# Moving every tap of a 31-tap depthwise convolution to the tensor engine, on its four groups of 32 columns

## The chip, the cores and the metric

The kernel runs on one core of one Trainium2 chip. A core has five engines with queues of their own: the tensor engine (PE, whose weight loads the profile lists apart as PEld), the vector engine (DVE), the scalar engine (ACT), the general engine (POOL) and the engine that only issues transfers (SP). The metric is device time in microseconds (us), and less is better.

## The reference

Two blocks run one after the other on 256 tokens of width 1024 (a state space mixer, a feed-forward part, an attention, a feed-forward part), and then a hybrid layer: its projections feed a low-rank attention and a convolution branch, and an output projection joins both. A layer of routed experts follows. The change touches the convolution branch of the hybrid layer alone, with 512 channels, 256 tokens and 16 learned tokens ahead of them:

```
CONV_CH = 512
CONV_K = 31
def conv_group(a, b, conv_w, conv_b, g_ln, b_ln):
    h = a * jax.nn.sigmoid(b)
    h = lax.conv_general_dilated(h, conv_w[:, None, :].astype(h.dtype), window_strides=(1,),
                                 padding=[(CONV_K - 1, 0)],
                                 dimension_numbers=('NWC', 'WIO', 'NWC'),
                                 feature_group_count=CONV_CH) + conv_b
    h = layernorm(h, g_ln, b_ln)
    return jax.nn.silu(h)
```

So each channel is a sum of 31 shifted copies of itself, each copy times a weight of that channel. Everything is in 32-bit floats.

## The kernel before

Weights stream from HBM in pieces of 128x1024 by SP (`weight`, L120). Each piece is split by ACT (L128) and DVE (L129) into two parts of type float32r, and a product with it is three products on PE (`mm_a`, L138 to L141, and `mm_b`, L143 to L147). Small products are plain f32: the trace shows each of these as two records on PE, one behind the other, each with a weight load.

The hybrid layer is `mix2` (L782). The 512 channels are four blocks `f` of 128 channels, one channel on each partition. `ab(f)` makes two items: the second puts `a * sigmoid(b)` into the tile `cu`, 30 zeros ahead of 272 tokens (L805 to L812). Then the 31 taps:

- `taps_pe` (L816) does some of them on PE: ACT writes the identity times a column of weights into a 128x128 tile `dg` (L821), and PE multiplies it with `cu`, shifted (L822). The tuple `PE_TAPS = (4, 4, 6, 31)` says how many for each block, 45 in all. ACT takes the sum out of PSUM with the bias into `cT` (L825).
- `taps_v` (L827) does the other 79 on DVE, one multiply-add of 128x256 each (L829).

The low-rank attention (`queries`, `key_values`, `attn_items`) goes head by head: `scores` (L964) on PE, a scaled minimum on DVE (L968), exponentials on ACT (L972, L973), `flip` (transposes on PE, L981, taken out by ACT, L983), `values` (L989). `attn_items` gives 50 items (16 of each of these three and two `attn_done`). `conv_done(t)` transposes `cT` to tokens on partitions and starts the layer norm. `norm_later` and `rstd_of` raise to the power -1/2 on POOL (L859, L154). `to_T` (L171) transposes the normed rows for `out_proj`, whose eight items `o` take the attention's rows in the first four and the convolution's in the last four.

In the attention of the block before, `scores` (L724) works on heads of 64 rows each: the two heads of a pair lie both on rows 0 to 63 or both on rows 64 to 127, and pairs on the one and the other half follow each other. The products of the expert router's scores (L1106) come four heads at a time on one half.

The code's order is a list with priorities: `run` emits items one after the other, `weave` spreads a list of side items between others by their number, and `defer` puts a step behind the items that follow. A planner then orders each engine's queue at compile time by that priority and by when it reckons an instruction's inputs to be there. So in the trace the instructions of neighbouring items are mixed. Each engine then works through its own queue in order. The order of the layer is written at its end:

```
run(low_rank() + B[0])
weave([queries] + B[1] + [key_values], C[0])
weave(S, B[2] + C[1] + B[3] + C[2])
load_gain("ffn2_g")
run(C[3])
flush()
o = out_proj(A["w_out2"], KD, mT, keep_tiles(sb, 3, "qT2"))
conv_done(0)
conv_done(1)
run(o[:4])
```

Here `B[f]` is `ab(f)`, `C[f]` the items of the convolution of block `f` (four taps each), and `S` the items of the attention.

Of the kernel before, what the change touches and what calls it, by code (L numbers as in the profile page):

```python
# [32 lines left out]
PE_TAPS = (4, 4, 6, 31)  # L33
# [13 lines left out]
for _n, _c in (("ssd_cw", 24 * 4), ("ssd_cb", 24), ("ffn_cw", 2 * FF * 3), ("ffn_cb", 2 * FF), ("c2w", 4 * CONV_K),  # L47
               ("c2b", 4), ("fox_qg", 1), ("fox_kg", 1), ("dt_bias", 1), ("a_log", 1), ("b_f", 1)):
    _cols(_n, _c)
# [17 lines left out]
def tile_body(ctx, tc, A, out):  # L67
# [13 lines left out]
    # ---- constants  # L81
# [35 lines left out]
    # ---- weights: load a piece, split it exactly in two parts of 12 significant bits  # L117
# [69 lines left out]
    def sum_sq(t, c, o, src, eps):  # L187
        # mean of squares of a row, in two halves
# [30 lines left out]
    def both_norms(t, c, acc):  # L219
        # the residual times the first block's last gain, the means of squares of both, and from these  # L220
        # 1 / rms of the first norm and the product of that with 1 / rms of the norm that follows it
# [12 lines left out]
    def keep_tiles(pool, n, *names):  # L234
        # made when first written; names: slots of tiles that are not read any more by then
        return [lambda name=name: pool.tile([P, 2, PIECE], F32R, name=name, bufs=1)
                for name in [*names, *(f"keep{j}" for j in range(n - len(names)))]]

    def out_proj(src, nk, yT, keep, fin=residual):
        """The last pieces are kept, so that the first tokens are done before the others."""  # L240
# [32 lines left out]
    def defer(f, n=1):  # L273
        """Emit a step after the n-th of the items that follow."""
        late.append([n, f])
# [8 lines left out]
    def flush():  # L284
        while late:
            tick()
# [6 lines left out]
    def weave(items, side, behind=False):  # L293
        """Emit a list of steps with a list of smaller ones spread between them, by their costs.

        behind: VectorE takes up the smaller ones only behind the split of the step's weights.
        """
# [17 lines left out]
    def causal(ps, acc, taps, cw, cb):  # L315
        # causal convolution along the tokens; the last tap has no shift
# [25 lines left out]
    def b_first(src, xT, pool, evac):  # L342
        """A block that begins on the first tokens while the others are still on their way."""
# [10 lines left out]
        def turn(f):  # L354
            # two of its four blocks of columns, columns on partitions
# [8 lines left out]
    def row_parts(pool, rows, name):  # L364
        # a table that is there twice, at partitions 0 and 32: its first part at 0, its second at 32
# [6 lines left out]
    def rowbc(ps, rows, r, more=None):  # L372
        # one row of a table in two parts, on all partitions; more: a tile to add
# [19 lines left out]
    # ---- layer 0: state space mixer  # L393
    def ssd():
        with ExitStack() as es:
# [47 lines left out]
            # large and negative where the position read comes after the position written  # L443
# [32 lines left out]
            def xs_items(g):  # L476
                # inputs of the recurrence, tokens on partitions
# [23 lines left out]
            def chain(g):  # L501
                hs = slice(8 * g, 8 * g + 8)
                # decay between every two positions of a chunk, transposed, times the masked products of B and C
# [21 lines left out]
                def state():  # L525
                    # state after the first chunk, read by the second
# [97 lines left out]
    def fox():  # L624
        with ExitStack() as es:
# [46 lines left out]
            # cum is minus the reference's sum  # L672
# [42 lines left out]
            def attend(hg):  # L715
# [3 lines left out]
                def scores(i, pr):  # L719
# [8 lines left out]
                    # minus the scores, and minus their maximum  # L728
# [53 lines left out]
    def mix2():  # L782
        with ExitStack() as es:
# [14 lines left out]
            # convolution branch: some of the taps on the tensor engine, as diagonal matrices  # L798
            cT = sb.tile([P, 4, T], F32, name="cT")
            U, CP = {}, {}  # L800

            def ab(f):
                pre = []

                def second():  # L805
# [4 lines left out]
                    U[f] = sb.tile([P, TM + CONV_K - 1], F32, name=f"cu{f}")  # L810
                    nc.vector.memset(U[f][:, :CONV_K - 1], 0.0)
                    nc.vector.tensor_tensor(U[f][:, CONV_K - 1:], pre[0], sg, op=OP.mult)  # L812
# [3 lines left out]
            def taps_pe(f, j0, j1):  # L816
                if j0 == 0:
                    CP[f] = ps_mm.tile([P, 512], F32, name="mm")[:, :T]
                dg = sb.tile([P, j1 - j0, P], F32, name="dg", bufs=2)
                for j in range(j0, j1):  # L820
                    nc.scalar.activation(dg[:, j - j0, :], ident, AF.Copy, scale=col("c2w", f * CONV_K + j))  # L821
                    nc.tensor.matmul(CP[f], lhsT=dg[:, j - j0, :], rhs=U[f][:, NM + j:NM + j + T], start=(j == 0),  # L822
                                     stop=(j == PE_TAPS[f] - 1))
                if j1 == PE_TAPS[f]:
                    nc.scalar.activation(cT[:, f, :], CP[f], AF.Identity, bias=col("c2b", f))  # L825

            def taps_v(f, j0, j1):  # L827
                for j in range(j0, j1):
                    nc.vector.scalar_tensor_tensor(cT[:, f, :], U[f][:, NM + j:NM + j + T], col("c2w", f * CONV_K + j),  # L829
                                                   cT[:, f, :], op0=OP.mult, op1=OP.add)  # L830

            def conv_items(f):
                n = PE_TAPS[f]
                return ([lambda j=j: taps_pe(f, j, min(j + 4, n)) for j in range(0, n, 4)]
                        + [lambda j=j: taps_v(f, j, min(j + 4, CONV_K)) for j in range(n, CONV_K, 4)])

            # low-rank query and key-value parts, tokens on partitions
# [13 lines left out]
            def norm_later(src, dst, g, n, then, half=False):  # L851
                # half: the source is twice the row that is meant
# [543 lines left out]
```

## Time and profile before

| what | value |
|---|---|
| median of 3 runs | 1768.36 us (1768.04 to 1769.67) |
| span of the profiled execution, first to last instruction | 1767.2 us |
| what lies around that span, as the difference from the median | 1.16 us |
| PE busy in it | 1728.7 us (98%) |
| DVE busy in it | 1244.6 us (70%) |
| ACT busy in it | 973.6 us (55%) |
| POOL busy in it | 35.2 us (2%) |

No time of its own is recorded for the profiled execution beside its span, so the difference from the median stands for what lies around it. A busy PE is not a PE at its peak: a record lasts longer than the distance to the next, since matmuls are pipelined. What one costs in a row of equal ones is read from the distance between their starts: the timeline merges equal neighbours, and (length of the merged row minus the length of one record) divided by (their number minus one) is that distance.

### The profile page before, as it was taken

How to read it: one execution, taken by the hardware profiler on the slowest of the kernel's cores; microseconds unless marked ns; L12 is line 12 of the kernel's file. 1: busy time of each engine (PE TensorE's matmuls, PEld its weight loads, DVE VectorE, ACT ScalarE, POOL GpSimd, SP SyncE). 2: the span in 40 equal slices, each digit the busy share in tenths (PEclk: the TensorE clock that was granted, in tenths of full speed). 3: DMA queues.
4: the chain of work that ended last, by engine and by line, in shares of the span. 5: the costliest groups of instructions: out<-in, count | busy, mean ns of one | idle time of the engine just before them, and what ended most of it. 6: DMA issues, size and time to landing. Idle time of an engine off the chain costs nothing.

```text
span 1767.2 us, 28831 instructions
## 1 busy us (share of the span) xinstructions
PE 1728.7 (98%) x11035; PEld 1536.4 (87%) x11035; DVE 1244.6 (70%) x2516; ACT 973.6 (55%) x1425; POOL 35.2 (2%) x45
## 2 busy tenths in 40 slices
PE   7999999999999999999999999999999999999998
PEld 6978779987777899878979999999999988888886
DVE  5777667765755677667877999977667666666665
ACT  5778546544465565457854544555555544444443
POOL 0000000000110000000000000000000000000000
PEclk9999999999999999999999999999999999999999
DMA  5534346665454465654245676754454577777774
GB/s 192 175 104 144 119 144 181 189 200 181 131 167 132 125 186 183 204 185 141 80 166 172 214 225 224 224 179 140 142 156 134 167 252 237 237 237 238 238 237 156
DMA packets 87578, 315.29 MB, mean 178 GB/s; under 512 B 9984, under 2 KB 10368, under 8 KB 87312
## 3 DMA queue, kind: packets, MB, share of 16 engines
q1 hardware_dynamic: 80352, 290.36, 52.8%
q10 hardware_dynamic: 7088, 23.09, 3.5%
q8 instruction: 86, 1.41, 0.3%
q14 instruction: 52, 0.43, 0.1%
HBM read 295.59 MB, written 17.83 MB: 177 GB/s over the span
## 4 chain that ended last, share of the span: by engine, by line
PE 91%; DVE 4%; ACT 1%; issue 1%; DMA 1%; POOL 1%; SPq 0%; DVEq 0%; POOLq 0%; ACTq 0%
PE mm L1254 20%; PE mm L139 13%; PE mm L141 13%; PE mm L140 13%; PE mm L146 7%; PE mm L145 7%; PE mm L147 7%; PE pst L1212 5%; DVE lo L129 1%; PE pst L171 1%; PE pst L546 1%; PE pst L724 1%; PE pst L375 1%; PE pst L377 1%; PE po L749 1%
## 5 line engine op out<-in xcount | busy, mean ns | idle before, releaser
L129 DVE TENSOR_TENSOR lo<-raw,hi 128x1024 fp32r<-128x1024 f32 (+1 forms) x492 | 599.9, 1220 | 341.7 <-PE mm L141 112.9
L128 ACT ACTIVATE hi<-raw 128x1024 fp32r<-128x1024 f32 (+1 forms) x492 | 519.3, 1057 | 526.0 <-PE mm L140 242.1
L139 PE MATMUL mm<-xT,hi 128*128 128x256 f32 (+1 forms) x1968 | 562.6, 286 | 1.2 <-DVE cacc L320 1.2
L141 PE MATMUL mm<-xT,lo 128*128 128x256 f32 (+1 forms) x1968 | 557.1, 283 | 1.5 <-DVE lo L129 1.5
L140 PE MATMUL mm<-xT,hi 128*128 128x256 f32 (+1 forms) x1968 | 552.0, 281 | 0.0
L139 PEld LDWEIGHTS mm<-xT,hi 128*128 128x128 f32 x1968 | 373.0, 190 | 5.0 <-issue 2.3
L141 PEld LDWEIGHTS mm<-xT,lo 128*128 128x128 f32 x1968 | 370.7, 188 | 2.6 <-DVE lo L129 2.2
L140 PEld LDWEIGHTS mm<-xT,hi 128*128 128x128 f32 x1968 | 371.8, 189 | 0.5
L1254 PE MATMUL mm<-hi,xT 128*128 128x512 f32 x992 | 270.0, 393 | 0.0
L1254 PEld LDWEIGHTS mm<-hi,xT 128*128 128x128 f32 x992 | 186.3, 188 | 42.6
L1254 PE MATMUL mm<-lo,xT 128*128 128x512 f32 x496 | 154.8, 393 | 0.0
L1254 PEld LDWEIGHTS mm<-lo,xT 128*128 128x128 f32 x496 | 93.1, 188 | 21.7 <-DVE lo L129 0.3
L145 PE MATMUL mm<-hi,xT 128*128 128x512 f32 (+1 forms) x240 | 96.3, 408 | 3.9 <-ACT xT L133 3.8
L1212 PE MATMUL pst<-oo 128*128 128x128 bf16 x768 | 99.4, 297 | 0.0
L147 PE MATMUL mm<-hi,xT 128*128 128x512 f32 (+1 forms) x240 | 95.0, 397 | 2.1 <-DVE xT L134 2.1
L146 PE MATMUL mm<-lo,xT 128*128 128x512 f32 (+1 forms) x240 | 96.1, 400 | 0.7 <-DVE lo L129 0.6
L1212 PEld LDWEIGHTS <-oo 128*128 128x128 bf16 x768 | 83.3, 118 | 3.4
L1214 ACT ACTIVATE G<-pst 128x512 f32<-128x512 f32 x64 | 71.1, 1111 | 16.4 <-PE pst L1212 16.4
L320 DVE SCALAR_TENSOR_TENSOR cacc<-mm,pcol,cacc 128x255 f32<-128x255 f32 (+1 forms) x144 | 68.4, 480 | 13.6 <-ACT cacc L317 11.2
L1204 DVE TENSOR_TENSOR oo<-oo,slot 128x1536 bf16<-128x1536 bf16 x64 | 60.2, 956 | 1.4
L145 PEld LDWEIGHTS mm<-hi,xT 128*128 128x128 f32 x240 | 45.5, 191 | 14.3 <-ACT xT L133 5.4
L147 PEld LDWEIGHTS mm<-hi,xT 128*128 128x128 f32 x240 | 45.5, 190 | 12.3 <-DVE xT L134 4.1
(404 smaller groups left out, 2095.7 us busy)
## 6 DMA issues: line engine op xcount, KB each, us to landing
raw<-in_u SPq DMA_DIRECT2D x128, 512.0 KB, 3.7
raw<-in_v SPq DMA_DIRECT2D x128, 512.0 KB, 4.2
raw<-in_w_up SPq DMA_DIRECT2D x88, 512.0 KB, 3.6
raw<-in_w_dn SPq DMA_DIRECT2D x44, 512.0 KB, 4.2
raw<-in_w_fox SPq DMA_DIRECT2D x32, 512.0 KB, 4.2
spill<-h ACTq DMA_DIRECT2D x30, 512.0 KB, 5.4
h<-spill SPq DMA_DIRECT2D x30, 512.0 KB, 4.7
raw<-in_w_xbc SPq DMA_DIRECT2D x24, 512.0 KB, 3.9
```

What stands on the lines that cost most here:

```text
L128: last[1] = nc.scalar.activation(hi[:, :width], raw[:, :width], AF.Copy)
L129: last[0] = nc.vector.tensor_tensor(lo[:, :width], raw[:, :width], hi[:, :width].bitcast(F32), op=OP.subtract)
L139: nc.tensor.matmul(ps, lhsT=hi[:, k, :], rhs=xT[:, k, 0, :], start=(k == 0), stop=False)
L140: nc.tensor.matmul(ps, lhsT=hi[:, k, :], rhs=xT[:, k, 1, :], start=False, stop=False)
L141: nc.tensor.matmul(ps, lhsT=lo[:, k, :], rhs=xT[:, k, 0, :], start=False, stop=(k == nk - 1))
L145: nc.tensor.matmul(ps, lhsT=xT[:, k, 0, c0:c1], rhs=whi, start=first, stop=False)
L146: nc.tensor.matmul(ps, lhsT=xT[:, k, 0, c0:c1], rhs=wlo, start=False, stop=False)
L147: nc.tensor.matmul(ps, lhsT=xT[:, k, 1, c0:c1], rhs=whi, start=False, stop=last)
L320: nc.vector.scalar_tensor_tensor(acc[:, d:], ps[:, :T - d], cw[:, j:j + 1], acc[:, d:], op0=OP.mult, op1=OP.add)
L1212: nc.tensor.matmul(pg[:, j, :], lhsT=oo[:, 1, :, j], rhs=oo[:, x, :, j], start=(x == 2), stop=(x == 4))
L1214: nc.scalar.activation(G[:, :, t0:t0 + NB].rearrange("p i t -> p t i"), pg, AF.Copy)
L1254: nc.tensor.matmul(acc[2 * t + c], lhsT=w[x][:, t * P:(t + 1) * P], rhs=y[:, c, :], start=(i == 0 and x == 0 and y is b[0]), stop=(i == P ...
```

## The change

All 31 taps of all four blocks go to PE. A block's 128 channels are cut into four groups `q` of 32. For each group a tile `cv` holds the 32 channels four times, on partitions 0 to 31, 32 to 63 and so on, each copy one token further on. One product with 128 rows and 32 columns of weights then adds up four neighbouring taps of 32 channels, and 8 of them (`NTAP`; the 32nd tap has weight zero) do the convolution of a group. The four groups write partitions 0, 32, 64 and 96 onwards of one PSUM tile, which puts them on the four groups of 32 columns of the array. The copies are made by writing `cu` to a tensor in HBM and reading it back, by transfers that POOL issues. The weights `dg` are 32 small diagonal blocks in a row, made by one multiplication on POOL for each block `f`. The side items in the attention are now `B[2]`, `C[0]`, `B[3]`, `C[1]`, `C[2]`, `C[3]`. The diff, cut to its core (the rest takes comments out):

```
-PE_TAPS = (4, 4, 6, 31)
+NTAP = 8
...
             cT = sb.tile([P, 4, T], F32, name="cT")
-            U, CP = {}, {}
+            UW = TM + CONV_K
+            eye = sb.tile([P, 32], F32, name="eye")
+            nc.vector.tensor_tensor(eye, ident[:, :32], ident[:, 32:64], op=OP.add)
+            for q in (64, 96):
+                nc.vector.tensor_tensor(eye, eye, ident[:, q:q + 32], op=OP.add)
+            U, V, DG = {}, {}, {}
...
-                    U[f] = sb.tile([P, TM + CONV_K - 1], F32, name=f"cu{f}")
-                    nc.vector.memset(U[f][:, :CONV_K - 1], 0.0)
-                    nc.vector.tensor_tensor(U[f][:, CONV_K - 1:], pre[0], sg, op=OP.mult)
+                    u = sb.tile([P, UW], F32, name="cu", bufs=2)
+                    nc.gpsimd.memset(u[:, :CONV_K - 1], 0.0)
+                    nc.gpsimd.memset(u[:, UW - 1:], 0.0)
+                    nc.vector.tensor_tensor(u[:, CONV_K - 1:UW - 1], pre[0], sg, op=OP.mult)
+
+                    d = dram.tile([P, UW], F32, name=f"cud{f}")
+                    nc.gpsimd.dma_start(d, u)
+                    V[f] = sb.tile([P, 4, UW - 3 - NM], F32, name="cv", bufs=2)
+                    for s in range(4):
+                        nc.gpsimd.dma_start(V[f][32 * s:32 * s + 32],
+                                            d[:, NM + s:UW - 3 + s].rearrange("(q c) t -> c q t", q=4))
+                    if f % 2 == 0:
+                        DG["tile"] = sb.tile([P, 2, 4 * NTAP, 32], F32, name=f"dg{f // 2}")
+                    DG[f] = DG["tile"][:, f % 2]
+                    nc.gpsimd.tensor_tensor(DG[f], eye[:, None].to_broadcast([P, 4 * NTAP, 32]),
+                                            col("c2w", 4 * NTAP * f, 4 * NTAP)[:, :, None]
+                                            .to_broadcast([P, 4 * NTAP, 32]), op=OP.mult)
...
-            def taps_pe(f, j0, j1):
...
-            def taps_v(f, j0, j1):
...
+            def taps(f):
+                pc = ps_t.tile([P, 512], F32, name="pst")[:, :T]
+                for m in range(NTAP):
+                    for q in range(4):
+                        nc.tensor.matmul(pc[32 * q:32 * q + 32], lhsT=DG[f][:, q * NTAP + m],
+                                         rhs=V[f][:, q, 4 * m:4 * m + T], start=(m == 0),
+                                         stop=(m == NTAP - 1))
+                nc.scalar.activation(cT[:, f, :], pc, AF.Identity, bias=col("c2b", f))
...
-                ln = sb.tile([P, 512], F32, name="ln", bufs=2)
+                ln = sb.tile([P, 768], F32, name="q2", bufs=2)[:, :512]
...
-            C = [conv_items(f) for f in range(4)]
+            C = [[lambda f=f: taps(f)] for f in range(4)]
             B = [ab(f) for f in range(4)]
             S = attn_items()
             run(low_rank() + B[0])
-            weave([queries] + B[1] + [key_values], C[0])
-            weave(S, B[2] + C[1] + B[3] + C[2])
+            run([queries] + B[1] + [key_values])
+            weave(S, B[2] + C[0] + B[3] + C[1] + C[2] + C[3])
             load_gain("ffn2_g")
-            run(C[3])
-            flush()
-            o = out_proj(A["w_out2"], KD, mT, keep_tiles(sb, 3, "qT2"))
             conv_done(0)
             conv_done(1)
+            flush()
+            o = out_proj(A["w_out2"], KD, mT, keep_tiles(sb, 3, "qT2", "dg0", "dg1"))
             run(o[:4])
```

## Rows read from the trace of the kernel before

**Rows 1.** Page, parts 1 and 2: whole span; 40 slices, busy and clock in tenths.

```profile
PE 1728.7 (98%) x11035; PEld 1536.4 (87%) x11035; DVE 1244.6 (70%) x2516; ACT 973.6 (55%) x1425; POOL 35.2 (2%) x45
...
PEclk9999999999999999999999999999999999999999
```

**Rows 2.** Windows of 10 us: busy time and instructions of each engine, clock, DMA.

```profile
850.00:860.00 10.00, 10.00 (x80) 9.71 (x80) 9.62 (x32) 7.66 (x30) 0.55 (x1) 1.00 0.10 27
...
870.00:880.00 10.00, 10.00 (x61) 8.64 (x61) 8.55 (x25) 8.60 (x30) 0.00 (x0) 1.00 0.00 0
```

**Rows 3.** Groups by line and form, 787 to 910 us: busy us, mean ns, idle before.

```profile
L829 DVE SCALAR_TENSOR_TENSOR cT<-cu,pcol,cT 128x256 f32<-128x256 f32 x79 | 37.4, 481 | 0.7
L822 PE MATMUL mm<-cu,dg 128*128 128x256 f32 x90 | 21.8, 382 | 0.0
...
L821 ACT ACTIVATE dg<-ident,pcol 128x128 f32<-128x128 f32 x45 | 15.1, 390 | 3.3 <-PE mm L822 3.3
```

**Rows 4.** Timeline of PE, 867 to 902 us: start, length, line, tiles, number.

```profile
867.65 0.49 PE L981 MATMUL pst<-ident,za 128*128 128x128 f32 x3
867.98 0.60 PE L822 MATMUL mm<-cu,dg 128*128 128x256 f32 x2
868.42 0.78 PE L989 MATMUL po<-v,pT 128*128 128x64 f32 x6
869.03 0.68 PE L964 MATMUL pst<-kT,qT 96*128 96x272 f32 x2
869.54 0.78 PE L989 MATMUL po<-v,pT 128*128 128x64 f32 x6
...
877.23 4.97 PE L822 MATMUL mm<-cu,dg 128*128 128x256 f32 x22
...
888.39 0.48 PE L145 MATMUL mm<-hi,mT 128*128 128x512 f32 x1
...
898.73 0.63 PE L171 MATMUL pst<-ident,on 128*128 128x128 f32 x4
```

**Rows 5.** Timeline of PE around products of 64 rows, in another layer.

```profile
560.58 0.60 PE L171 MATMUL pst<-ident,o 128*128 128x128 f32 x4
561.11 0.72 PE L724 MATMUL pst<-qkT,qkT 64*128 64x128 f32 x8
561.87 0.50 PE L145 MATMUL mm<-hi,oT 128*128 128x512 f32 x1
```

**Rows 6.** The same view, eight such records on one half of the rows.

```profile
942.19 1.16 PE L1106 MATMUL pst<-keys,qT 64*128 64x128 f32 x8
```

**Rows 7.** The line L724, 560.5 to 562 us: record ns, first and last start.

```profile
L724 PE MATMUL pst<-qkT,qkT x8: 272/272/373, 561.1 to 561.6; 64*128 64x128 f32 x8
```

**Rows 8.** POOL's groups by form over the span.

```profile
L154 POOL TENSOR_TENSOR rstd<-ms,nhalf 128x8 f32<-128x8 f32 x8 | 13.0, 1645 | 79.0 <-DVE ms L152 60.5 <-ACT cumr L368 18.5
...
L859 POOL TENSOR_TENSOR nr<-nss,nhalf 128x1 f32<-128x1 f32 x9 | 6.2, 698 | 89.3 <-DVE nss L858 74.4 <-DVE rtmp L848 14.0 <-DVE rtmp L845 0.8
...
L84 POOL IOTA jmp<- 128x128 f32 x1 | 0.2, 238 | 0.4 <-POOLq L1388 0.4
```

**Rows 9.** Transfers issued from 780 to 930 us: number, KB each, us to landing.

```profile
save<-h ACTq DMA_DIRECT2D x2, 512.0 KB, 2.6
...
gain<-in_rowp ACTq DMA_DIRECT2D x1, 512.0 KB, 4.7
...
rope<-in_rope ACTq DMA_DIRECT2D x1, 48.0 KB, 1.8
```

**Rows 10.** Timeline of ACT: what it takes to issue one transfer.

```profile
841.89 0.33 ACTq L110 DMA_DIRECT2D gain<-in_rowp  x1
```

**Rows 11.** Timeline of POOL: the last norm of the attention.

```profile
880.78 0.72 POOL L859 TENSOR_TENSOR nr<-nss,nhalf 128x1 f32<-128x1 f32 x1 [21.79 <-DVE nss L858]
```

More of the change, by code (lines that the diff above doesn't have):

```diff
@@ L44, in _cols @@
     PCOLS[name] = (sum(c for _, c in PCOLS.values()), n)
-for _n, _c in (("ssd_cw", 24 * 4), ("ssd_cb", 24), ("ffn_cw", 2 * FF * 3), ("ffn_cb", 2 * FF), ("c2w", 4 * CONV_K),
+for _n, _c in (("ssd_cw", 24 * 4), ("ssd_cb", 24), ("ffn_cw", 2 * FF * 3), ("ffn_cb", 2 * FF), ("c2w", 16 * NTAP),
                ("c2b", 4), ("fox_qg", 1), ("fox_kg", 1), ("dt_bias", 1), ("a_log", 1), ("b_f", 1)):
@@ L809, in second @@
                     nc.vector.tensor_scalar(sg, sg, 0.5, 0.5, op0=OP.mult, op1=OP.add)
-                    U[f] = sb.tile([P, TM + CONV_K - 1], F32, name=f"cu{f}")
-                    nc.vector.memset(U[f][:, :CONV_K - 1], 0.0)
-                    nc.vector.tensor_tensor(U[f][:, CONV_K - 1:], pre[0], sg, op=OP.mult)
-                return [lambda: pre.append(a_block(A["w_ab"][f, 0], xT)), second]
-            def taps_pe(f, j0, j1):
[L817 to L825, printed above, removed]
@@ L827, in taps_v @@
-            def taps_v(f, j0, j1):
[L828 to L835, printed above, removed]
+                    u = sb.tile([P, UW], F32, name="cu", bufs=2)
@@ L1359, in _layout @@
     put("ffn_cb", g["ffn_conv_b"].reshape(2, FF, P).transpose(2, 0, 1))
-    put("c2w", g["conv_w_2"][0].reshape(CONV_K, 4, P).transpose(2, 1, 0))
+    w = np.concatenate([g["conv_w_2"][0].reshape(CONV_K, 512), np.zeros((1, 512), np.float32)])
+    put("c2w", w.reshape(NTAP, 4, 16, 32).transpose(1, 3, 2, 0).reshape(P, -1))
     put("c2b", g["conv_b_2"][0].reshape(4, P).T)
```

## The prediction

> **What bounds the kernel now.** I read the page first, then windows of the stage, then its groups, then the timeline of PE. The page says that PE is busy 98% of the span at full clock, DVE 70%, ACT 55% and POOL 2% [rows 1]. That is an average over six layers, so the stage itself has to be read: the tensor engine's part of the hybrid layer lies between 820 and 890 us. Two of its windows stand for it [rows 2]: PE is busy for all 10.00 us of each while DVE is at 9.62 and 8.55 and ACT at 7.66 and 8.60. So PE sets the pace here, with DVE close behind, and a transfer is scarce (a DMA share of 0.10 and 0.00).
>
> The groups show where the convolution sits [rows 3]: 79 multiply-adds on DVE for 37.4 us, 45 diagonals made by ACT for 15.1 us, and 90 records on PE for its 45 taps. The reader is to see the last figure of each: the idle time before these groups is 0.7, 0.0 and 3.3 us, and ACT's 3.3 are waits for PE. Nobody of weight waits for DVE or ACT. So the 37 us that DVE loses and the 15 that ACT loses are worth nothing by themselves; only records on PE are.
>
> What a record costs on PE is a distance and not a length. In the timeline 22 records of L822 take 4.97 us [rows 4]; one lasts 0.38 [rows 3], so their starts are (4.97 - 0.38) / 21 = 0.219 us apart. The 90 cost 90 x 0.219 = 19.7 us.
>
> **The change part by part.** *Removed from PE:* these 19.7 us. *Removed from DVE and ACT:* the above, at nothing, since PE's own work covers them; were PE not the bound, it would be up to 37 us.
>
> *Added on PE:* 4 blocks x 8 products x 4 groups x 2 records = 256 records of 256 columns. The trace has no product on a group of 32 columns, so the price is bounded from both sides. Above, one after the other at the distance of L822: 256 x 0.219 = 56.1 us. Below, four at once: a quarter, 14.0 us. Which it is can't be read for column groups, but it can for row groups. Eight records on the same half of the rows take 1.16 us [rows 6], so with a record of 0.272 [rows 7] the last starts 0.89 after the first, 0.127 apart. Eight records of the same form on two halves, four and four, take 0.72 [rows 5], so the last starts 0.45 after the first. One after the other it would be 0.89. If the second half had only begun beside the last record of the first, it would be 3 x 0.127 + 3 x 0.127 = 0.76. At 0.45 both halves began together and each ran its four records side by side with the other. I take the lower end, four at once, because this is the nearest row: same type, two records per product, another cut of the same array.
>
> A page of the Trainium skill speaks against it: "TensorE: Matmul & The Clock Gate", Part 3, says that matmuls are strictly first in, first out, in start and in end. For row groups the trace disagrees, as 0.45 against 0.76 us shows; no run here shows column groups, so it stays a rival below. The same section gives 2.38 times the speed for three column groups; at the same share four would be 3.2 times, and by that my estimate of the records alone is 17.7 us in place of 14.0.
>
> *Going to narrow groups and back* costs PE a pause. In front of the products of 64 rows the last transpose starts at 560.58 + 0.60 - 0.27 = 560.91 and the next record at 561.11: 0.20 where transposes are (0.60 - 0.27) / 3 = 0.11 apart. From there to the next full product are 0.76 us [rows 5], and four records side by side at 0.127 are 0.51. So an excursion costs 0.09 + 0.25 = 0.34 us. Four blocks make four: 1.4 us. Now the planner breaks such a row up where an earlier step becomes ready, as it does now (two records of L822 between transposes and `values` [rows 4]). Bounds: no break, and four in each block (16 x 0.34 = 5.4 us). I take one in each: 1.4 us.
>
> *Moved to POOL:* for each block two fills, one multiplication of 128x1024 and five transfers; POOL issued no transfer before. The multiplication: POOL writes 128x128 in 0.238 us, and a power of 128x8 takes 1645 ns against 698 for 128x1 [rows 8], 0.135 us per column. So it lies between 8 x 0.238 = 1.9 us and 1024 x 0.135 = 139 us; a product is no power, so I take the lower end, about 2 us. "GPSIMD Engine Reference" of the Trainium skill, section 3.1, has 4497 ns for 2048 elements of such a sum, an estimate of 2.2 us here. A transfer: ACT issues one in 0.33 us [rows 10], POOL's slowest instruction takes 1.65 [rows 8]; landing 1.8 to 4.7 us for 48 to 512 KB [rows 9], and these are 155 KB (the write) and 145 KB (each read). I take 1 and 3 us, so `cv` is there about 1 + 3 + 4 + 3 = 11 us after `cu`. For block 0 the queries, block 1 and the keys lie between, for block 1 some 25 of the 50 attention items. What waits behind on POOL are the powers of `norm_later`. For the attention's second norm the row shows POOL idle for 21.79 us ahead of it [rows 11], so that one has room. All of it costs nothing as long as PE has other work.
>
> *The tight place* is block 3. `cv` has two buffers, so the reads for block 3 wait on POOL until PE is through with block 1. Then they take between 4 x 0.33 + 1.8 = 3.1 and 4 x 1.65 + 4.7 = 11.3 us. PE's cover meanwhile: 12 items of attention are about four heads, each 0.33 for three transposes (867.65 to 867.98), 0.61 for `values` (868.42 to 869.03) and 0.51 for `scores` (869.03 to 869.54) [rows 4], 5.8 us; block 2 with 14.0 / 4 + 0.34 = 3.8; together 9.6. So between nothing and 1.7 us of wait; at my values, 4 + 3 = 7, nothing.
>
> *Moved at the end:* the norm of the convolution now comes ahead of the output projection in the list. Before, PE had 898.73 - 888.39 = 10.3 us of projection before the first transposes of the normed convolution [rows 4]. The planner places by readiness, so the same matmuls are still there to fill it: nothing, and up to 10.3 us if it kept the list's order.
>
> Two small things go with this, both at nothing. The block's sum now takes one of three PSUM buffers from `scores` and `flip` for some 4 us; they keep two, and one head needs one of each. And two of the projection's kept weight pieces now lie where `dg` was, so the last is split only when block 3 is through; it is read behind the 10.3 us of projection above.
>
> *The sum:* -19.7 + 14.0 + 1.4 + 1.4 = -2.9 us. Made against the profiled execution: 1767.2 - 2.9 = 1764.3 of span, and with the 1.16 us around it 1765.5 us, as much as the median of 1768.36 less 2.9. The likeliest case's own range: no excursions at all and no break, -5.7, gives 1762.7; with 5.4 for breaks and 1.7 of wait, +2.8, it is 1771.2.
>
> **The rivals.** *One group at a time.* Then the change doesn't do what it says on PE: 56.1 + 2.8 - 19.7 = +39.2, 1807.6 us. For it: no row shows column groups at work side by side, and these share all 128 rows, while the halves in [rows 5] share none. Against it: the array is cut in the other direction without trouble.
>
> *Two at a time.* The two records of a product use the same column group, so the second waits for the first; in a queue that keeps its order, only the first record of the next product runs beside it. Then 256 / 2 x 0.219 = 28.0, and 28.0 + 2.8 - 19.7 = +11.1: 1779.5 us. It decides as soon as the queue to the columns is one queue. For it: all four groups read the same rows, and what the trace shows is queues by rows.
>
> *The copies come late.* One mechanism, on the side of slower: POOL holds the reads of block 3 until block 1 is through. If a transfer costs POOL 3 us to issue, 4 x 3 + 3 = 15 us stand against 9.6 of cover: 5.4 of wait, and the sum is +2.5. With 4 us each it is 19 - 9.6 = 9.4, the sum +6.5, 1774.9 us. It decides from (9.6 + 2.9 - 3) / 4 = 2.4 us per issue, where the gain is eaten. For it: POOL has no transfer in the trace to go by. Against it: nothing on POOL now is longer than 1.65 us.
>
> *Longer uninterrupted rows*, which end faster: the -5.7 of the range.
>
> **How the numbers follow.** A change under 0.2%, 3.5 us, is about what a measurement of this kernel can't tell from none: 1764.8 to 1771.9 are the same. Four at once without a serious wait: 0.60, because of [rows 5, 6]. Late copies: 0.11. Two at a time: 0.13. One at a time: 0.16. Of the first, 0.32 lie under 1764.8, since its range is centred near 1766 and a part of the breaks may not occur, 0.25 within and 0.03 above; late copies give 0.03 within and 0.08 above; the other two are slower. Faster 0.32, same 0.28, slower 0.40. The time predicted is that of the likeliest, 1765.5 us. The range from 1761.5 to 1780.5 takes in that case, the late copies and two at a time (0.84 with their tails cut: about 0.8), and leaves out one at a time.
>
> **What would show it.** Four at once: 64 records of a block with starts 0.05 to 0.06 us apart on average, and 14 to 17 us between the first and last starts of all four blocks' records together, other work taken off. Two at a time shows 0.11, one at a time 0.22. No attention instruction inside a block means no breaks. The copies in time: no wait of PE for a transfer into `cv`, and POOL's issues near 1 us. The end: projection matmuls of the first four items between the convolution's transposes and those of its norm. DVE's share in 850 to 880 should drop from 9 tenths to about 5 without PE ending earlier for it. I am wrong if PE in this stage did wait for DVE in a way that these windows hide, or if the planner, which doesn't know the real time of POOL's transfers, puts a block ahead of its copies with other work behind it.

## The result, and the profile after

The changed kernel takes 1783.21 us (median of 4 runs, 1780.74 to 1784.11) against 1769.01 us of the kernel before in the same comparison: a ratio of 1.0084, 95% interval 1.0069 to 1.0098. It is slower by 14.2 us, and lies outside the predicted range. A ratio is told from all runs of a kernel and a profile from one of them, which in two cases below lies 1.8 us under and 3.3 us over their median.

The page's first part and five windows of the changed kernel (10 us each; busy us and instructions of PE, PEld, DVE, ACT and POOL, then the granted clock, the transfers' share and GB/s):

```profile
PE 1727.9 (97%) x11201; PEld 1530.0 (86%) x11201; DVE 1218.7 (69%) x2436; ACT 961.5 (54%) x1380; POOL 55.0 (3%) x77
```

```profile
790.00:800.00 10.00, 6.05 (x27) 5.28 (x26) 7.66 (x12) 1.42 (x4) 9.08 (x5) 0.74 0.34 117
...
850.00:860.00 10.00, 10.00 (x114) 7.98 (x114) 3.58 (x14) 6.11 (x20) 2.75 (x5) 1.00 0.42 125
870.00:880.00 10.00, 10.00 (x130) 7.18 (x121) 2.47 (x8) 5.36 (x15) 2.20 (x4) 1.00 0.39 112
...
890.00:900.00 10.00, 1.98 (x9) 1.64 (x10) 5.27 (x11) 3.19 (x7) 1.65 (x3) 0.69 0.11 42
900.00:910.00 10.00, 9.31 (x30) 7.20 (x30) 4.28 (x5) 3.59 (x5) 0.00 (x0) 0.63 0.27 65
```

The two windows of [rows 2] look as forecast, and more so: PE is busy throughout, and DVE falls from 9.62 and 8.55 to 3.58 and 2.47, where about half was forecast. The loss lies at the two ends of the layer. In 790 to 800 PE is busy 6.05 us while POOL is busy 9.08, and in 890 to 900 PE is busy 1.98. In both the granted clock averages about 0.7, so PE is for a part of them at the lower of its two levels (1.2 in place of 2.4 GHz).

To see this in numbers the layer is cut in three by PE's starts: the head from the first product of `low_rank` (128x416, 791.28 us before) to the first `scores`, the middle to the last `values`, the end to the last record of the output projection. The instructions ahead of the layer are the same in all these kernels, but their profiles begin it between 786.95 and 792.39 us, without the layer's doing; so lengths are compared and not places.

| kernel, us | head | middle | end | layer | median or ratio to before |
|---|---|---|---|---|---|
| before | 46.59 | 39.25 | 34.71 | 120.55 | 1769.01 |
| changed | 50.69 | 42.27 | 42.65 | 135.61 | 1.0084 |

The layer is 15.06 us longer, near the 14.2 us of the runs. (The rest of the program, which is the same in all these kernels, takes between 1642.6 and 1647.7 us in their profiles; so the layer tells more than the span.) Before, 42 records of the convolution still stood in the end; so the middle is longer by itself, and middle and end are read together.

Groups of the changed kernel between 786 and 925 us (busy us, mean ns, idle before):

```profile
L839 PE MATMUL pst<-cv,dg 128*32 128x256 f32 x256 | 14.6, 380 | 0.0
L824 POOL DMA_DIRECT2D cv<-cud x16 | 8.8, 555 | 11.7 <-DMA cud<-cu 5.8 <-PE pst L839 3.2 <-PE pst L988 2.6
L829 POOL TENSOR_TENSOR dg<-eye,pcol 128x1024 f32<-128x1024 f32 x4 | 8.5, 2133 | 3.8 <-DVE eye L804 3.8
```

On PE the convolution is now busy for 14.6 us in place of 21.8 [rows 3]. The head shows up in the timelines of POOL, DVE and PE, 790 to 800 us (start, length, line; in brackets the idle time before and what ended it):

```profile
790.65 1.92 POOL L829 TENSOR_TENSOR dg<-eye,pcol 128x1024 f32<-128x1024 f32 x1 [3.81 <-DVE eye L804]
792.53 0.70 POOL L232 TENSOR_TENSOR stat<-stat,nhalf 128x2 f32<-128x2 f32 x1
793.20 6.54 POOL L829 TENSOR_TENSOR dg<-eye,pcol 128x1024 f32<-128x1024 f32 x3
...
793.26 4.70 DVE L209 SCALAR_TENSOR_TENSOR hn<-h,stat,gain 128x512 f32<-128x512 f32 x2 [2.31 <-POOL stat L232]
798.00 2.28 DVE L789 TENSOR_SCALAR h<-h,stat 128x1024 f32<-128x1024 f32 x1
...
795.80 1.09 PE L171 MATMUL pst<-ident,hn 128*128 128x128 f32 x4 [3.07 <-DVE hn L209]
```

The same place in the kernel before:

```profile
795.12 1.41 DVE L209 SCALAR_TENSOR_TENSOR hn<-h,stat,gain 128x512 f32<-128x512 f32 x2 [0.65 <-POOL stat L232]
...
796.02 0.63 PE L171 MATMUL pst<-ident,hn 128*128 128x128 f32 x4 [0.22 <-DVE hn L209]
```

In the changed kernel the power of the layer norm (L232) begins at 792.53, when the first multiplication lets POOL go, though DVE had delivered its input by 790.71. Then three multiplications run beside DVE, and DVE's two L209 take 2.39 us each, where they took 0.75 before. PE waits 3.07 us for the first, where it waited 0.22.

The end is in the timelines of DVE and PE, 883 to 903 us:

```profile
883.38 0.75 DVE L869 SCALAR_TENSOR_TENSOR on<-o,nr,row_oattn_g 128x512 f32<-128x512 f32 x1 [0.69 <-POOL nr L866]
...
885.02 1.21 PE L1024 MATMUL pst<-ident,cT 128*128 128x128 f32 x8
...
887.92 0.63 PE L145 MATMUL mm<-hi,mT 128*128 128x512 f32 x2
894.07 1.08 PE L171 MATMUL pst<-ident,on 128*128 128x128 f32 x4 [5.53 <-DVE on L869]
899.11 1.94 PE L171 MATMUL pst<-ident,on 128*128 128x128 f32 x8 [3.95 <-DVE on L869]
901.73 0.79 PE L145 MATMUL mm<-hi,mT 128*128 128x512 f32 x1 [0.69 <-ACT mT L133]
902.32 0.63 PE L146 MATMUL mm<-lo,mT 128*128 128x512 f32 x1
902.75 0.63 PE L145 MATMUL mm<-hi,mT 128*128 128x512 f32 x1
```

Where [rows 4] had 10.3 us of projection in one piece, PE gets through a few records up to 887.92 and waits 5.53, 3.95 and 0.69 us. The first four transposes are of the convolution's norm; the eight at 899.11 hold those of the attention's second norm. The rows of that norm were ready on DVE at 884.13 (first line), 15 us earlier: it was not their input that these transposes waited for, but their place in PE's queue (the run with one number changed, below, bears this out). At the lower clock the records behind them start 0.43 us apart.

### The profile page after: what moved, and what is told of

Read it like the earlier page. It is cut to its first block, busy times and chain, and to the rows that moved or that the text cites. A ratio compares the mean times of both kernels' runs of the same rounds, so it can differ in the third digit from the quotient of the medians.

```text
span 1778.7 us, 29104 instructions
## 1 busy us (share of the span) xinstructions
PE 1727.9 (97%) x11201; PEld 1530.0 (86%) x11201; DVE 1218.7 (69%) x2436; ACT 961.5 (54%) x1380; POOL 55.0 (3%) x77
## 4 chain that ended last, share of the span: by engine, by line
PE 91%; DVE 4%; ACT 1%; issue 1%; DMA 1%; POOL 1%; SPq 0%; DVEq 0%; POOLq 0%; ACTq 0%
PE mm L1260 20%; PE mm L139 13%; PE mm L141 13%; PE mm L140 12%; PE mm L146 7%; PE mm L145 7%; PE mm L147 7%; PE pst L1218 5%; PE pst L171 1%; DVE lo L129 1%; PE pst L839 1%; PE pst L546 1%; PE pst L724 1%; PE pst L375 1%; PE pst L377 1%
## 5 line engine op out<-in xcount | busy, mean ns | idle before, releaser
L1260 PEld LDWEIGHTS mm<-lo,xT 128*128 128x128 f32 x496 | 93.1, 188 | 21.8 <-DVE lo L129 0.4
```

The lines of the kernel that those rows point to most:

```text
L1260: nc.tensor.matmul(acc[2 * t + c], lhsT=w[x][:, t * P:(t + 1) * P], rhs=y[:, c, :], start=(i == 0 and x == 0 and y is b[0]), stop=(i == P ...
```

## The experiments

The theory after this result: two losses, one at each end, and a gain on PE that is as predicted. The rivals: the end is lost by the projection's new place in the list, or by the copies; the head is lost by the queue of POOL alone.

**The old order of the end.** The changed kernel with

```
+            flush()
+            o = out_proj(A["w_out2"], KD, mT, keep_tiles(sb, 3, "qT2", "dg0", "dg1"))
             conv_done(0)
             conv_done(1)
-            flush()
-            o = out_proj(A["w_out2"], KD, mT, keep_tiles(sb, 3, "qT2", "dg0", "dg1"))
```

> The changed kernel with the end of the layer in the order of before: the deferred norms first, the output projection made, then the two conv_done, then the projection's items. Theory 1, the new order of the end leaves PE without projection work while the convolution's norm runs (PE is busy only 1.98 of 10 us from 890 to 900): the time falls by 10 to 13 us, to about 1771. Rival, the copies through HBM or the attention set the end, and the order of the list does not matter because the planner reorders: within 2 us of 1783. A third reading, the lost clock after the idle stretch is most of it: the fall would be about 3 us.

Measured: 1770.76 us, ratio 1.0020 (1.0011 to 1.0030). The layer takes 125.29 us, of which the end is 32.09 in place of 42.65; the head stays at 50.94. That is theory 1.

**The multiplications on DVE.** The changed kernel with

```
-                    nc.gpsimd.tensor_tensor(DG[f], eye[:, None].to_broadcast([P, 4 * NTAP, 32]),
+                    nc.vector.tensor_tensor(DG[f], eye[:, None].to_broadcast([P, 4 * NTAP, 32]),
...
```

> The changed kernel with the four multiplications that make dg on the vector engine in place of POOL. Theory 2, these multiplications on POOL delay the layer's first norm, by holding POOL's queue and by slowing DVE's instructions from 0.75 to 2.35 us while they run: the time falls by 3 to 5 us, to about 1779, and the idle stretch of PE between 793 and 798 us is gone. Rival, PE waits there for weights or transfers: no change, 1783.

Measured: 1777.37 us, ratio 1.0050 (1.0035 to 1.0066); head 45.53, end 42.37, layer 130.17. One multiplication takes 1.22 us on DVE, and L209 is back at 748 ns. That is theory 2, with 5.4 us in the layer in place of 3 to 5.

**Both of these edits.**

> Both edits at once. If the two losses are all that stands against the gain on PE, the time is 1783 - 12 - 4 = 1767, 2 us under the kernel before, near the 1765.5 that was predicted without them. If the copies through HBM cost something of their own, it stays 4 us or more above the kernel before.

Measured: 1765.45 us, ratio 0.9990 (0.9981 to 0.9999); head 45.42, middle 42.26, end 30.57, layer 118.25. The two losses are then 135.61 - 118.25 = 17.4 us, and what is left of the change is 2.3 us less than before. It needs nothing else to explain the result. The losses taken alone, 10.3 and 5.4 us, are 1.6 us less than that: with the old end alone the end takes 32.09 us and not 30.57, behind the same waits but at a lower granted clock (see the last section).

**The multiplications on POOL, but later**, ordered behind the powers of the low-rank norms (L866) by

```
-                    nc.gpsimd.tensor_tensor(DG[f], eye[:, None].to_broadcast([P, 4 * NTAP, 32]),
...
+                    with tc.issue_after(last_pow[0].ins):
+                        nc.gpsimd.tensor_tensor(DG[f], eye[:, None].to_broadcast([P, 4 * NTAP, 32]),
...
```

> The changed kernel with the multiplications still on POOL, but ordered behind the powers of the low-rank norms. If the loss is POOL's queue, which holds the power of the layer's first norm behind a multiplication, this is as good as moving them to DVE: about 1779. If the loss is that DVE runs slower while POOL multiplies, the multiplications slow DVE at the new place too, where PE waits less for DVE: between 1779 and 1783, and DVE instructions beside them take two to three times as long as otherwise.

Measured: 1779.1 us, ratio 1.0066 (1.0051 to 1.0082); head 47.32, middle 43.91 (42.27 in the changed kernel). L209 is free now, but not what DVE does beside the multiplications. POOL and DVE of this kernel:

```profile
808.44 5.70 POOL L831 TENSOR_TENSOR dg<-eye,pcol 128x1024 f32<-128x1024 f32 x3
...
808.48 0.28 DVE L134 TENSOR_TENSOR ckT<-pst,ckT 128x128 fp32r<-128x128 f32 x1
808.68 1.71 DVE L858 TENSOR_TENSOR kr<-kr,rtmp 128x16 f32<-128x16 f32 x1
810.31 0.41 DVE L134 TENSOR_TENSOR cqT<-pst,cqT 128x256 fp32r<-128x256 f32 x1
810.64 0.28 DVE L134 TENSOR_TENSOR ckT<-pst,ckT 128x128 fp32r<-128x128 f32 x1
810.84 1.53 DVE L871 SCALAR_TENSOR_TENSOR ck<-z,nr,row_gkv 128x128 f32<-128x128 f32 x1
...
813.37 1.59 DVE L129 TENSOR_TENSOR lo<-raw,hi 128x768 fp32r<-128x768 f32 x1
...
858.09 1.90 POOL L831 TENSOR_TENSOR dg<-eye,pcol 128x1024 f32<-128x1024 f32 x1
858.15 2.40 DVE L871 SCALAR_TENSOR_TENSOR on<-o,nr,row_oattn_g 128x512 f32<-128x512 f32 x1 [0.68 <-POOL nr L868]
...
860.60 0.66 PE L171 MATMUL pst<-ident,on 128*128 128x128 f32 x4 [1.54 <-DVE on L871]
```

A multiplication is 5.70 / 3 = 1.9 us long, so the three end at about 810.3, 812.2 and 814.1. The first three slow DVE instructions (their like take 0.16, 0.34 and 0.95 us elsewhere in the same stage) end at 810.39, 812.37 and 814.96: each begins inside a multiplication and ends behind that one's end by no more than its own usual length. The fourth multiplication does the same to the product of the attention's first norm (2.40 us in place of 0.75), and PE waits 1.54 us for that: this is the longer middle. L134 between them, which reads PSUM, takes its usual 0.28 and 0.41. So these DVE instructions aren't slowed down, they are shut out until POOL's instruction ends; what the slow ones share is that both their inputs lie in SBUF. The Trainium skill says this under "SBUF — State Buffer", section "Who interferes with whom": DVE and GpSimd share a pair of ports to SBUF, which is an exclusive lock; a DVE instruction with two inputs in SBUF contends with a GpSimd instruction that reads SBUF, and one with at most one input there, outside the fast modes that use both pairs of ports, does not. The trace agrees for the first kind and for L134 (1.71 and 1.53 against 0.28 us). For a single tensor in SBUF it shows the other case too: L789 in the head takes 2.28 us beside the last multiplication, 0.75 without; whether that is such a fast mode, no run here shows. The prediction didn't look for such a rule.

**The same with the old end.**

> The old order of the end, and the four multiplications on GpSimd but behind the powers of the low-rank norms. Theory, that a multiplication on GpSimd stops VectorE's instructions on SBUF wherever it stands: about 3.5 us over the version with both undone, 1769 us. Rival, that only the layer norm's power, queued behind the multiplications, was the loss: as the version with both undone, 1765.5 us.

Measured: 1771.14 us, ratio 1.0035 (1.0023 to 1.0048). The layer is 121.84 us, 3.6 over the version with both edits, as the theory of the lock had it; the runs say 4.5 parts in a thousand more, 8 us. The profiled run took 1769.32 us, 1.8 under the median, so part of the 4 us between these two lies in the runs without a profile; the rest stays open.

**The list emptied once more**, ahead of the convolution's norms: in the changed kernel

```
+            flush()
             conv_done(0)
             conv_done(1)
             flush()
```

> The changed kernel with one more call that empties the list of delayed steps, ahead of the convolution's norms; these still stand ahead of the output projection. Theory: what the end loses comes from the attention's transposes, which are delayed by three items and so fall behind the convolution's transposes when no items lie between; with them in front, nearly all of the 12.4 us that the old order of the end gave back comes back: about 1771 us. Rival: it comes from the projection standing behind the convolution's norms in the list; then this changes little, about 1781 to 1783 us.

Measured: 1771.87 us, ratio 1.0029 (1.0018 to 1.0041); end 30.57, layer 124.72. The projection still stands behind the convolution's norms, and the loss is gone; so the projection's place was not it.

**The new order of the end alone**, in the kernel before:

> The kernel before with the new order of the end alone (the convolution's norms, then the delayed steps, then the output projection), and its convolution as it was. Theory: the loss of the end belongs to the order alone, 10 to 13.5 us: 1778 to 1781 us. Rival: it needs the new convolution, whose last block is through later on PE or earlier on VectorE: then about 1768 us.

Measured: 1767.89 us, ratio 1.0003 (0.9994 to 1.0013); layer 120.58 against 120.55. The theory as written falls: alone, the order costs nothing. PE of this kernel shows why:

```profile
881.61 0.63 PE L171 MATMUL pst<-ident,on 128*128 128x128 f32 x4 [0.23 <-DVE on L862]
882.07 4.48 PE L822 MATMUL mm<-cu,dg 128*128 128x256 f32 x20
886.39 0.49 PE L1017 MATMUL pst<-ident,cT 128*128 128x128 f32 x3
```

The attention's transposes (L171) are ready while 20 records of the last block are still to come, and the planner puts them between. In the changed kernel their rows were ready at 884.13, 0.89 us ahead of the convolution's transposes, and they found no such place; that the shortness of the block is the reason is a reading of these two traces and not tested by itself. What the runs show is that the order and the short block cost together what neither does alone (the short block with the old order: an end of 30.57 us).

**One number.** The transposes of the attention's norm are delayed by three items of the list. In the new order no items lie between, so the delay runs out only in the emptying, behind the convolution's own steps, which have a delay of none. The changed kernel with

```
-                norm_later(o, on, og, 3, lambda a: to_T(a, 4, mT, i * P))
+                norm_later(o, on, og, 1, lambda a: to_T(a, 4, mT, i * P))
```

> The changed kernel with one number changed: the transposes behind the attention's norm are delayed by one item and no longer by three; the convolution's norms still come first, then the delayed steps, then the projection. Theory: the loss at the end is these transposes standing behind the convolution's own in the list, so it goes, 12 us in the stretch from the attention's last product to the projection's last (42.65 us in the changed kernel, about 30.6 here): about 1771 us. Rival: the emptying ahead of the convolution's norms did more than this order: 1776 to 1783 us.

Measured: 1771.71 us, ratio 1.0025 (1.0014 to 1.0035); end 30.04, layer 124.29. PE of this kernel:

```profile
889.73 1.21 PE L1024 MATMUL pst<-ident,cT 128*128 128x128 f32 x8
890.78 0.60 PE L171 MATMUL pst<-ident,on 128*128 128x128 f32 x4
...
902.43 0.63 PE L171 MATMUL pst<-ident,on 128*128 128x128 f32 x4
```

Everything stands as in the changed kernel, but the attention's transposes follow the convolution's first ones at once, and PE has the projection of the second token block's attention to do until the next ones at 902.43. The number alone is worth 135.61 - 124.29 = 11.3 us in the layer, and 42.65 - 30.04 = 12.6 in the end. (It holds for the attention's first norm too; the middle is 0.64 us longer with it, 42.91.)

**The loops of a block exchanged**, in the version with both edits (old end, multiplications on DVE), all eight products of a column group before the next group:

```
-                for m in range(NTAP):
-                    for q in range(4):
+                for q in range(4):
+                    for m in range(NTAP):
```

> The version with both undone (old end, multiplications on VectorE), with the two loops of the block exchanged: all eight products of one column group, then those of the next. Theory: what runs four at once are records next to each other in PE's queue, and PE starts them in the queue's order; then a group's 16 records follow one another at 0.216 us and a block takes 64 x 0.216 = 13.8 us in place of 3.66, four blocks 40.7 us more: about 1806 us. Rival: a waiting record doesn't hold back those of other groups behind it: 3.66 us per block, about 1765.5 us.

Measured: 1795.91 us, ratio 1.0167 (1.0147 to 1.0187); layer 151.14. A block on PE:

```profile
846.25 11.50 PE L839 MATMUL pst<-cv,dg 128*32 128x256 f32 x64
```

Neither number held. One at a time, 63 x 0.216 + 0.38 = 14.0 us were to be seen (the expectation's 13.8, with the last record's length), and 3.66 with free choice. It is 2.5 us under the first, which is 12 records of 0.216: at each of the three changes of group some four records of the old and the new one ran side by side. So PE's records do start beside waiting ones of another group, but only from a few places behind them. The single records of the trace put a number to it: the first record of a new group starts when three of the old one are still waiting. With the groups inside it is the same, if a product's two records stand one behind the other in the queue: the first records of the four groups start within 0.02 us, past three waiting second ones, and the next four follow 0.216 us later. So what stands ahead of the prediction, "Each engine then works through its own queue in order", is not strictly so for PE: in these two kernels a record starts past three waiting ones of other groups, and none past more. The order with the groups inside is worth 11.50 - 3.66 = 7.8 us per block.

**Every read issued twice**, in the version with both edits:

```
-                    for s in range(4):
+                    for s in (0, 1, 2, 3, 0, 1, 2, 3):
```

> The version with both undone, with the four reads of each block issued twice: 8 issues of 0.55 us on GpSimd in place of 4, and twice the bytes. Theory: the copies have time to spare; block 3's reads are issued by 869.84 us and its products start at 877.61, so 2.2 us more are hidden: 1765.5 us. Rival: a copy that lands later holds PE up, 2.2 us for each block or for the last alone: 1768 to 1774 us.

Measured: 1773.07 us, ratio 1.0040 (1.0026 to 1.0054); layer 128.20. The theory of spare time failed as stated. The wait is not where the rival had it either. POOL, DVE and PE of this kernel:

```profile
856.71 0.56 POOL L866 TENSOR_TENSOR nr<-nss,nhalf 128x1 f32<-128x1 f32 x1 [1.13 <-DVE nss L865]
...
860.59 0.44 DVE L818 TENSOR_TENSOR cu<-mm,sg 128x272 f32<-128x272 f32 x1
860.95 0.74 DVE L869 SCALAR_TENSOR_TENSOR on<-o,nr,row_oattn_g 128x512 f32<-128x512 f32 x1
...
861.75 0.66 PE L171 MATMUL pst<-ident,on 128*128 128x128 f32 x4 [2.17 <-DVE on L869]
```

POOL's power is done at 857.27, but DVE comes to the product with it (L869) only at 860.95, behind `cu`. With single reads it came to it at 858.13, ahead of `cu`. So the planner has put it later in DVE's queue, and PE waits 2.17 us for it. Presumably it reckoned with the doubled reads ahead of that power on POOL. The middle is 6.1 us longer than with single reads (48.33 against 42.27): waits of 2.17 and 0.62 us, and a granted clock of 0.66 from 860 to 870. The end is 3.9 us longer (34.49), with waits of 0.57, 2.71 and 0.69 us and a clock of 0.83 from 902 to 912. None of these waits is for a transfer. That a changed order costs PE a wait is shown; that the end's 3.9 us come that way too is not.

**No copies at all**, in the version with both edits. The products read the block's own `cu` in place of `cv`, which leaves the shifts between the four copies out; PE's records are as many and as long:

```
-                    d = dram.tile([P, UW], F32, name=f"cud{f}")
...
+                    V[f] = u
...
```

> The version with both undone, without the copies: no write to cud and no reads into cv, the products read the block's own cu in place of cv, with as many rows, columns and records as before. What the taps compute is left wrong. Theory: the copies cost nothing where they stand, since the doubled reads lost their time by the new order that the planner chose for them: within 0.1% of the version with both undone, 1765.5 us, layer 118 us. Rival: the copies set when the blocks can start, and that costs already with single reads: 2 to 6 us less, 1760 to 1763.5 us.

Measured: 1764.45 us, ratio 0.9985 (0.9976 to 0.9995); layer 117.85 against 118.25. So the copies cost 0.4 us, next to nothing: the theory held.

**Versions meant to be faster.** In the version with both edits, the multiplications on DVE ordered behind the writing of `cu`:

```
...
-                    nc.vector.tensor_tensor(DG[f], eye[:, None].to_broadcast([P, 4 * NTAP, 32]),
...
+                    with tc.issue_after(cu.ins):
+                        nc.vector.tensor_tensor(DG[f], eye[:, None].to_broadcast([P, 4 * NTAP, 32]),
...
```

> The version with both undone, its multiplications on VectorE ordered behind the writing of cu of the same block, so that they leave the stretch from 794 to 803 us. Theory: there PE's waits for VectorE (0.55 and 0.32 us and what follows from them) shrink, up to 1 us: 1764.5 us. Rival: at their new places they hold up the rotations of the queries or the splits of the weights as much: 1765.5 us or more.

Measured: 1764.57 us, ratio 0.9987 (0.9977 to 0.9996). The head falls from 45.42 to 43.88 as meant, but the end takes 32.17 in place of 30.57, and the layer stays (118.33). The profiled run took 1767.88 us, 3.3 over the median, at a granted clock of 0.995 on average, where eight of the ten have 0.997 or 0.998; so this longer end need not be the others'. With the blocks moved forward in the list as well,

```
-            weave(S, B[2] + C[0] + B[3] + C[1] + C[2] + C[3])
+            weave(S, B[2] + C[0] + C[1] + B[3] + C[2] + C[3] + [lambda: None])
```

> The version with the multiplications behind cu, with the convolution's blocks spread earlier between the attention's items, so that the last block is through before the attention is. Theory: the end waits 1.54 us because the norm of the convolution takes 12.7 us from its transposes to the next, longer than the projection beside it; with an earlier start the wait and the lower clock behind it (0.78 and 0.88) go: 2 to 3.5 us less in the layer, 1761 to 1763 us. Rival: the chain behind the attention's own norm becomes the wait in its place: about 1764.5 us.

Measured: 1772.46 us, ratio 1.0035 (1.0020 to 1.0049); layer 127.00. The rival's wait came, but at a higher price than it gave: PE waits for the attention's own norm with nothing left beside it.

```profile
891.71 1.09 PE L171 MATMUL pst<-ident,on 128*128 128x128 f32 x4 [5.73 <-DVE on L870]
```

Last, the changed kernel with only the delay of one and the multiplications on DVE behind `cu`:

> The changed kernel with two edits: the delay of one item, and the multiplications on VectorE behind the writing of cu. Theory: the two losses add up and are all that there is, so this ends where the version with the old end and the same multiplications does: 1764.5 us, layer 118.3 us. Rival: the new order of the end has a price of its own, beside the delay: 1767 us or more.

Measured: 1764.31 us, ratio 0.9982 (0.9973 to 0.9992); head 43.95, middle 42.91, end 30.23, layer 117.09. Its layer is the shortest of all; its ratio can't be told from that of the version with the multiplications behind `cu` (0.9987). The new order of the end shows no price beside the delay.

## Why the prediction was wrong

*What bounds the kernel* was right for the middle: PE. From 850 to 880 us DVE fell from 27.7 to 11.5 us of 30 and ACT from 24.1 to 18.5, and PE stayed busy throughout. But PE's part of the layer was taken to lie between 820 and 890 us; it lasts from 791 to 912, and both losses lie in what this left out.

*Added on PE*, four at once: right. A block's 64 records take 3.66 us, so their starts are (3.66 - 0.38) / 63 = 0.052 us apart, where 0.05 to 0.06 was to show it; from first to last start the four blocks take 4 x 3.28 = 13.1 us together (14 to 17 was forecast). Both rivals with fewer at a time fall. *Breaks* were charged with 1.4 us, and there are none: each block is one row of 64. *Going to narrow groups and back* was charged with 0.34 us a block; by the starts around a block it is about 0.2 (an estimate: 0.09 ahead of its first record, 0.11 behind its last four).

*The sum*, -2.9: near, once the two failed steps are taken out, and partly by luck. The version with both edits is 2.3 us shorter in the layer, that with two others 3.5. The breaks' 1.4 us never came, and in their place PE waits 1.54 and 0.69 us at the end of the version with both edits, where the kernel before waits 0.23.

*Moved to POOL*: its sizes were right, its price wrong. A multiplication takes 1.9 us alone and 2.13 on average (about 2 was taken), an issue 0.55 (1 taken), a landing 3.0 to 3.1 in the median (3 taken). But "all of it costs nothing as long as PE has other work" failed. Leaving POOL gave 135.61 - 130.17 = 5.4 us with the new end and 125.29 - 118.25 = 7.0 with the old one. 5.2 and 5.5 us of these are in the head (50.69 against 45.53, 50.94 against 45.42), where the layer norm's power stands behind a multiplication and L209 is shut out; the middle is the same, and the rest of the 7.0 is the end at the lower clock. The prediction looked at the powers of `norm_later` alone, and at no instruction of DVE. With the multiplications behind the powers 3.6 us remain (121.84 against 118.25), 1.9 in the head and 1.6 in the middle.

*The tight place* and *the copies come late*: right that they don't cost. Block 3 begins at 881.43, when its last read was issued by 873.7, and the kernel without copies is 0.4 us shorter.

*Moved at the end* is the larger failure: taken at nothing, "up to 10.3 us if it kept the list's order", and 11.3 measured. The reason given, that the planner places by readiness and so the same matmuls are there to fill, overlooked what the matmuls hang on. The first four items need the attention's transposes for the second token block; those had slipped behind the convolution's norm by a delay counted in items. It also failed on readiness itself: the transposes' input was ready at 884.13, and they ran at 899.11. The bound was nearly right, and the likeliest case's own range (up to 1771.2 us) didn't take it in: no rival carried it. By it alone the sum would have been -2.9 + 10.3 = +7.4, 1775.8 us; with the price of POOL between 1781 and 1783.

## What to carry to other kernels

When a long row of products is made short, look for what was ready only because of it: here transposes that used to find their place inside the row lost it, and a delay counted in list items put them behind the next chain. Work moved to an idle engine costs what it shuts out: name the instructions that run beside it and where their inputs lie, and not only that engine's queue. When a bound of the working ("up to 10.3") hangs on how a planner will decide, give it a chance of its own.

## What was not expected of the hardware

Records of different column groups start 0.052 us apart on average when they alternate, though each product's two records use the same group: in fours within 0.02 us, and 0.216 us from one four to the next. With the groups one behind the other only four records of the old and four of the new group overlap at each change (11.50 us for 64).

A DVE instruction with both inputs in SBUF waits out a multiplication on POOL (0.16 us becomes 1.71), one with an input in PSUM doesn't (0.28). POOL pays as well: beside the two L209 a multiplication takes up to 2.36 us in place of 1.90.

The clock turned on little. In the version with both edits PE waits 1.54 us in the end and the granted clock stays at 1.00 in the 10 us behind it. In the one with the old end alone, and in that with the multiplications behind `cu`, the same wait of 1.54 us comes with 0.83 from 895 to 905 us, and the end takes 32.1 and 32.2 us in place of 30.57. With the loops exchanged it comes too (0.83 from 925 to 935 us), and in the version with the list emptied once more and that with POOL's later multiplications and the old end it doesn't (1.00, waits of 1.54 and 1.55 us). What decides between the two isn't settled.
